# A log-sum-exp kernel: block-ordered rows and one closing store for the last batch, late sums in its last tiles, one common store for the other batches

## The chip, the cores and the metric

The kernel runs on one core of one Trainium2 chip. The metric is the device time of one execution in microseconds (us). Twelve executions of the kernel before gave a median of 335.04 us, from 333.62 to 335.29. The profiled execution took 334.2 us, of which the span from the first to the last profiled instruction is 332.4 us; the 1.8 us between the two lie outside the profile.

## What is computed

The input x has 8 batches of 2048 rows of 2048 floats, 134 MB in all. A row holds 8 heads of 256 values; a bias (8 x 256) is added; for each row and head the output is log(sum(exp(x + bias))), and each result is written twice in a row.

```python
x_heads = x.reshape(B, S, H, Dh).transpose(0, 2, 1, 3)
x_heads = x_heads + bias[None, :, None, :]
x_tiled = np.repeat(x_heads, 2, axis=2)
mx = x_tiled.max(axis=-1, keepdims=True)
lse = mx.squeeze(-1) + np.log(np.exp(x_tiled - mx).sum(axis=-1))
```

The output is 8 x 8 x 4096 floats, 1.05 MB. The kernel does not subtract the maximum; it sums exp(x + bias), or exp(x) * exp(bias), directly.

## The kernel before

**Tiles.** A tile is 256 rows of one batch as 128 partitions x K = 2 rows x 2048 columns, 2 MB. There are T = 64 tiles, eight per batch, and nine buffers `xt`. Tile t lives in buffer t mod 9. `rows_of` (L94) gives partition p the two neighbouring rows 2p and 2p + 1, one run of 16 KB in memory, except in the very last tile, where row k of partition p is row k * 128 + p. `load` (L102) issues the load from the SP queue. `next_waiting` (L340) calls it for tile t + 9 once tile t has been read.

**Stages.** `STAGES` (L27) sets how a tile's eight heads are split, and whether the load and the work go by whole tiles or by halves of 1 MB (one row k at a time):

- tiles 0 to 48, BULK: heads 0 and 1 by the TensorE path, heads 4 to 7 by the GpSimd path, heads 2 and 3 by a weight; whole tiles
- tiles 49 to 56, MIXED: head 0 by TensorE, heads 1 to 4 by weights, heads 5 to 7 by GpSimd; whole tiles
- tiles 57 to 60: MIXED in halves
- tiles 61 to 63, PROMPT: heads 0 and 1 by TensorE, heads 2 to 7 by weights, nothing on GpSimd; in halves

The last tile is cut further by `LAST_CUTS` (L29): its first half is one piece; its second half has pieces of columns 0 to 1024, 1024 to 1536 and 1536 to 2048.

**Paths.** On the TensorE path `add_bias` (L159) puts the bias into PSUM with one matmul of a row of ones (L166), adds the tile with a matmul against the identity (L171), and `sum_biased` (L174) lets ScalarE take exp and sum over each head (L177, an ACTIVATE and an ACTIVATION_READ_ACCUMULATOR per head). On the GpSimd path `g_add` (L195) adds the bias in place, ScalarE takes exp (L200), and VectorE sums (L216). On the weight path ScalarE takes exp of x alone (L200), and `weigh` (L228) multiplies by exp(bias) and sums, one instruction pair per head on VectorE; BULK does the same with one multiplication for two heads (L210) ahead of the reduction.

**Order of the work.** The order is written out by hand: the main loop (L302) issues, for each piece, the TensorE work and the GpSimd addition, then what `waiting` holds of the piece before (its exp and VectorE sums of the GpSimd heads, and the load of tile t + 9), then the exp of the weighted heads, the sums of its TensorE heads, and the weighing. Each engine runs its instructions in the order of issue. DMA issues from SP rotate over eight completion semaphores, and an issue waits until the DMA eight issues earlier has landed.

**Ends of batches.** The sums of a batch lie in `R[b]` (rows on partitions). `finish_batch` (L283) transposes them with TensorE (L244, two transposes into `tpair`), takes Ln into one of two buffers `res` (L257; the repetition comes from reading each value twice), and stores 64 partitions x 2 KB (128 KB) from the SP queue (L278). It runs two tiles after the batch's last tile, and stands in the same SP queue as the loads. The last batch is finished in four parts: tiles 56 to 61 (`R7`: 48 rows, eight stores of 12 KB from the GpSimd queue), tile 62 (`Ry`, 16 KB), and each half of tile 63 (`Rz`, 8 KB each), the last after everything else (L356).

Of the kernel before, what the change touches and what calls it, by code (L numbers as in the profile page):

```python
# [9 lines left out]
F32 = mybir.dt.float32  # L10
BF16 = mybir.dt.bfloat16
ACT = mybir.ActivationFunctionType
# [3 lines left out]
K = 2  # L16
# [9 lines left out]

STAGES = [(0, BULK, False), (49, MIXED, False), (57, MIXED, True), (61, PROMPT, True)]  # L27

LAST_CUTS = [[0, 2048], [0, 1024, 1536, 2048]]  # L29


@with_exitstack
def kernel(
# [6 lines left out]
    nc = tc.nc  # L40
    P = nc.NUM_PARTITIONS
    B, S, D = x.shape
    H, Dh = bias.shape
    assert D == H * Dh and S % (P * K) == 0
    NBLK = S // (P * K)
    T = B * NBLK
    CPE = 2 * Dh
    MM = 512
# [3 lines left out]
    sb = ctx.enter_context(tc.tile_pool(name="sb", bufs=1))  # L52
# [7 lines left out]
    ident = sb.tile([P, P], F32, name="ident")  # L60
    ones = sb.tile([1, P], F32, name="ones")
    ones3 = sb.tile([3, P], BF16, name="ones3")
    b3 = sb.tile([3, CPE], BF16, name="b3")
    bparts = sb.tile([1, 3, CPE], BF16, name="bparts")
    brest = sb.tile([1, 2, CPE], F32, name="brest")

    nblk = [NBLK] * (B - 1) + [NBLK - 2]
    R = [sb.tile([P, K, H, nblk[b]], F32, name=f"R{b}") for b in range(B)]
    Ry = sb.tile([P, K, H], F32, name="Ry")
    Rz = sb.tile([P, K, H], F32, name="Rz")  # L70
    junk = [sb.tile([P, Dh], F32, name=f"junk{i}") for i in range(2)]
    res = [sb.tile([H * NBLK, P, K, 2], F32, name=f"res{i}") for i in range(2)]
    xts = [sb.tile([P, K, D], F32, name=f"xt{i}") for i in range(NBUF)]
    w_ps = pp.tile([P, W1 - W0], F32, name="w_ps")
    ps = [pp.tile([P, MM], F32, name=f"ps{i}") for i in range(5)]
# [1 line left out]
    tps = [tpair[:, i] for i in range(2)]  # L77

    def mode_of(t):
        return [m for t0, m, _ in STAGES if t0 <= t][-1]  # L80
# [4 lines left out]
    def pieces(t):  # L85

        if not halves_of(t):
            return [(0, K, 0, D)]
        cuts = [[0, D]] * K if t < T - 1 else LAST_CUTS
        return [  # L90
            (k, k + 1, c0, c1) for k in range(K) for c0, c1 in zip(cuts[k], cuts[k][1:])
        ]

    def rows_of(t):  # L94

        b, blk = divmod(t, NBLK)
        v = x[b, blk * P * K : (blk + 1) * P * K, :]
        if t < T - 1:
            return v.rearrange("(p k) d -> p k d", k=K)
        return v.rearrange("(k p) d -> p k d", k=K)  # L100

# [10 lines left out]
    for set_idx, (_name, funcs) in enumerate(get_activation_tables(nc.m.arch).items()):  # L112
        if ACT.Exp in funcs and ACT.Ln in funcs:
            nc.scalar.add_instruction(
                mybir.InstLoadActFuncSet(
                    name=nc.get_next_instruction_name(),
# [27 lines left out]
    for i, c in enumerate(range(G0, D, MM)):  # L144
        spread(ps[i], c, c + MM)
        nc.scalar.activation(  # L146
            out=b_rep[:, c - G0 : c - G0 + MM], in_=ps[i], func=ACT.Copy
# [8 lines left out]
    n_ps = [0]  # L156
    n_junk = [0]

    def add_bias(m, views):  # L159

        n = m["pe"] * Dh
        got = []
        for v in views:
            p = ps[n_ps[0] % len(ps)]
            n_ps[0] += 1
            nc.tensor.matmul(  # L166
                p[:, 0:n], lhsT=ones3, rhs=b3[:, 0:n], start=True, stop=False
            )
            got.append(p)
        for p, v in zip(got, views):  # L170
            nc.tensor.matmul(p[:, 0:n], lhsT=ident, rhs=v, start=False, stop=True)  # L171
        return got

    def sum_biased(m, p, dst):  # L174
        for h in range(m["pe"]):
            c = h * Dh
            nc.scalar.activation(  # L177
                out=p[:, c : c + Dh],
                in_=p[:, c : c + Dh],
                func=ACT.Exp,  # L180
                accum_out=dst(h),
            )

    def each_row(src, c, n, k_rows):

        return bass.AP(
            tensor=src.tensor,
            offset=src.offset + c,
            ap=[src.ap[0], [0, k_rows], [1, n]],
        )  # L190

    def g_add(m, xt, k0, k1):
        c = m["g0"] * Dh
        v = xt[:, k0:k1, c:D]
        nc.gpsimd.tensor_tensor(  # L195
            out=v, in0=v, in1=each_row(b_rep, c - G0, D - c, k1 - k0), op=ALU.add
        )

    def exp_inplace(v):
        nc.scalar.activation(out=v, in_=v, func=ACT.Exp)  # L200
# [22 lines left out]
    def weigh(v, h, dst):  # L223
        c = h * Dh
        w = w_ps[:, c - W0 : c - W0 + Dh] if c < W1 else w_sb[:, c - W1 : c - W1 + Dh]
        j = junk[n_junk[0] % 2]
        n_junk[0] += 1
        nc.vector.tensor_tensor_reduce(  # L228
            out=j,
            in0=v,  # L230
            in1=w,
            scale=1.0,
            scalar=0.0,
            op0=ALU.mult,
            op1=ALU.add,
            accum_out=dst,
        )

    def finish(b, src, n_blk, k_rows, base, i, engine):

        nr = H * n_blk
        n = P * k_rows * 2
        for k in range(k_rows):
            nc.tensor.transpose(out=tps[i][0:nr, k], in_=src(k), identity=ident)  # L244
        tp = tps[i]
        rs = res[i]
        tv = bass.AP(
            tensor=tp.tensor,
            offset=tp.offset,
            ap=[[tp.ap[0][0], nr], [1, P], [P, k_rows], [0, 2]],  # L250
        )
        rv = bass.AP(
            tensor=rs.tensor,
            offset=rs.offset,
            ap=[[rs.ap[0][0], nr], [2 * k_rows, P], [2, k_rows], [1, 2]],
        )
        nc.scalar.activation(out=rv, in_=tv, func=ACT.Ln)  # L257

        if n_blk == 1:
            step, parts = 2 * S, [H]  # L260
        elif n_blk == NBLK:
            step, parts = n, [nr]
        else:
            step, parts = n, [n_blk] * H
        r0 = 0
        for rows in parts:
            h, m = divmod(r0, n_blk)
            ov = bass.AP(
                tensor=out.tensor,
                offset=out.offset + (b * H + h) * 2 * S + 2 * base + m * n,  # L270
                ap=[[step, rows], [1, n]],
            )
            iv = bass.AP(
                tensor=rs.tensor,
                offset=rs.offset + r0 * rs.ap[0][0],
                ap=[[rs.ap[0][0], rows], [1, n]],
            )
            engine.dma_start(out=ov, in_=iv)  # L278
            r0 += rows
        assert r0 == nr  # L280


    def finish_batch(b, engine):  # L283
        finish(
            b,
            lambda k: R[b][:, k].rearrange("p h n -> p (h n)"),
            nblk[b],
            K,
            0,
            b % 2,  # L290
            engine,
        )

    def sums_of(t):

        b, blk = divmod(t, NBLK)
        if t < T - 2:
            return R[b][:, :, :, blk]
        return Ry if t < T - 1 else Rz

    waiting = None
    for t in range(T):  # L302
        m = mode_of(t)
        xt = xts[t % NBUF]
        sums = sums_of(t)
        with_pool = m["g0"] < H
        for k0, k1, c0, c1 in pieces(t):
            if t == T - 1 and c1 == D and k0 > 0:

                finish(  # L310
                    B - 1,
                    lambda k: Rz[:, k0 - 1],
                    1,
                    1,
                    S - (K - k0 + 1) * P,
                    0,
                    nc.sync,
                )
            if c0 == 0:
                got = add_bias(m, [xt[:, k, 0 : m["pe"] * Dh] for k in range(k0, k1)])  # L320
                if with_pool:
                    g_add(m, xt, k0, k1)

            if waiting:
                waiting()
            h0 = max(c0 // Dh, m["pe"])
            h1 = min(c1 // Dh, m["g0"])
            if h0 < h1 and not m["late"]:
                exp_inplace(xt[:, k0:k1, h0 * Dh : h1 * Dh])
            if c0 == 0:  # L330
                for k in range(k0, k1):
                    sum_biased(m, got[k - k0], lambda h: sums[:, k, h : h + 1])
            if not m["late"]:
                for k in range(k0, k1):
                    for h in range(h0, h1):
                        weigh(
                            xt[:, k, h * Dh : (h + 1) * Dh], h, sums[:, k, h : h + 1]
                        )

            def next_waiting(t=t, m=m, xt=xt, k0=k0, k1=k1, sums=sums):  # L340
                if m["g0"] < H:
                    later(m, xt, k0, k1, sums)
                if k1 == K and t + NBUF < T:
                    load(t + NBUF)

            waiting = next_waiting
            if t == T - 1 and c0 == 0:
                if k0 == 0:
                    finish_batch(B - 1, nc.gpsimd)
                elif k0 == 1:  # L350
                    finish(B - 1, lambda k: Ry[:, k], 1, K, S - 2 * K * P, 0, nc.sync)

        fb, at = divmod(t - 2, NBLK)
        if fb >= 0 and at == NBLK - 1:
            finish_batch(fb, nc.sync)
    finish(B - 1, lambda _: Rz[:, K - 1], 1, 1, S - P, 1, nc.sync)  # L356

    order.__exit__(None, None, None)

# [29 lines left out]
```

## Time and profile before

| | |
|---|---|
| profiled execution | 334.2 us; span 332.4 us |
| median of 12 executions | 335.04 us (333.62 to 335.29) |
| VectorE busy | 288.6 us, 87% of the span |
| ScalarE busy | 291.7 us, 88% |
| GpSimd busy | 274.6 us, 83% |
| TensorE busy | 229.2 us, 69%, at a mean granted clock of 0.73 |
| DMA | 135.43 MB at a mean of 407 GB/s; HBM read 134.23 MB, written 1.05 MB |
| chain that ended last | DMA 65%, ScalarE 15%, TensorE 10%, GpSimd 4% of the span |

A busy share is an average over the whole span, so it says nothing of what limits a given stage. The chain that ended last is followed back from the last instruction, each time to what released the waiting instruction. Wherever it says "DMA xt<-in_x_dram", an engine had been waiting for a load; a long chain of engine lines means that the engines followed one another with no load to wait for. In timelines, the number in brackets is the idle time ahead of an instruction, and the arrow names what ended it. The profile's trace also keeps every DMA packet (its start, its duration and its size) and the time at which each of the 16 DMA engines reported its share of a transfer as landed.

### The profile page before, as it was taken

The numbers are of one execution on the slowest core, as the hardware profiler recorded it, in microseconds if no ns is written. First come the engines' busy times: TensorE is split into PE (matmuls) and PEld (weight loads), VectorE is DVE, ScalarE is ACT, GpSimd is POOL, SyncE is SP. The second block draws the span as 40 slices with busy tenths as digits, with TensorE's granted clock in tenths as the row PEclk, the third lists the DMA queues.
The fourth block names the chain that finished last, engine by engine and source line by source line (L and its number), as shares of the span: only waits on it lengthen the run. The fifth ranks groups of instructions, "written<-read, shape, count | busy, mean of one in ns | idle before, by whom it ended". The sixth has DMA issues, their size and how long they took to land.

```text
span 332.4 us, 2370 instructions
## 1 busy us (share of the span) xinstructions
PE 229.2 (69%) x412; PEld 71.8 (22%) x412; DVE 288.6 (87%) x380; ACT 291.7 (88%) x570; POOL 274.6 (83%) x87
## 2 busy tenths in 40 slices
PE   6496774796766766776968856778774554665981
PEld 2122221221221221221222221121122232222220
DVE  0029999999999999899989999999899999999992
ACT  2279999899999999989899999998999987899893
POOL 7999989998989999999898999988997766876204
PEclk9999777559798769877595789865876555555576
DMA  7999999999999999999999999999999999999940
GB/s 293 436 436 420 433 424 432 432 422 432 425 429 425 430 426 425 436 425 428 429 428 424 434 426 430 428 426 433 428 424 431 428 428 428 413 422 420 421 175 17
DMA packets 11489, 135.43 MB, mean 407 GB/s; under 512 B 1609, under 2 KB 1625, under 8 KB 2513
## 3 DMA queue, kind: packets, MB, share of 16 engines
q1 hardware_dynamic: 11120, 135.17, 96.1%
q0 software_dynamic: 352, 0.10, 0.2%
q14 instruction: 12, 0.10, 0.1%
q8 instruction: 3, 0.05, 0.1%
q10 hardware_dynamic: 2, 0.01, 0.0%
HBM read 134.23 MB, written 1.05 MB: 407 GB/s over the span
## 4 chain that ended last, share of the span: by engine, by line
DMA 65%; ACT 15%; PE 10%; POOL 4%; issue 2%; DVE 2%; POOLq 0%; DVEq 0%; SPq 0%; ACTq 0%
DMA xt<-in_x_dram 63%; ACT xt L200 10%; PE ps L171 8%; ACT ps L177 5%; POOL xt L195 3%; DMA b<-bparts 2%; PE ps L166 1%; DVE R L216 1%; DVE xt L210 1%; DMA brow<-in_bias_dram 1%; DMA out_dram<-res 0%; PE tpair L244 0%; DVE junk L228 0%; POOL brest L131 0%; POOL brest L133 0%
## 5 line engine op out<-in xcount | busy, mean ns | idle before, releaser
L195 POOL TENSOR_TENSOR xt<-xt,b_rep 128x2048 f32<-128x2048 f32 (+2 forms) x65 | 264.2, 4066 | 36.3 <-DMA xt<-in_x_dram 30.1
L171 PE MATMUL ps<-xt,ident 128*128 128x512 f32 (+1 forms) x256 | 174.7, 819 | 76.9 <-DMA xt<-in_x_dram 75.5
L200 ACT ACTIVATE xt<-xt 128x3072 f32<-128x3072 f32 (+3 forms) x89 | 184.8, 2095 | 11.4 <-POOL xt L195 11.1
L216 DVE TENSOR_REDUCE R<-xt 128x12 f32<-128x3072 f32 (+2 forms) x65 | 186.0, 2861 | 5.8 <-DVE xt L210 1.0
L177 ACT ACTIVATE ps<-ps 128x256 f32<-128x256 f32 x232 | 85.6, 369 | 16.1 <-PE ps L171 11.7
L171 PEld LDWEIGHTS ps<-xt,ident 128*128 128x128 f32 x256 | 59.2, 259 | 157.4 <-DMA xt<-in_x_dram 115.5
L210 DVE TENSOR_TENSOR xt<-xt,w_ps 128x1024 f32<-128x1024 f32 x49 | 59.6, 1217 | 30.0 <-ACT xt L200 29.8
L166 PE MATMUL ps<-b,ones 3*128 3x512 bf16 (+1 forms) x128 | 48.2, 449 | 8.3 <-ACT ps L177 4.8
L177 ACT ACTIVATION_READ_ACCUMULATOR ps<-ps 128x1 f32 x232 | 44.1, 190 | 0.0
L228 DVE CUSTOM_DVE_ANT_0 junk<-xt,w_ps 128x256 f32<-128x256 f32 x114 | 40.6, 415 | 2.6 <-ACT xt L200 2.5
L166 PEld LDWEIGHTS <-ones 3*128 3x128 bf16 x128 | 8.0, 98 | 72.2 <-issue 72.2
L278 POOL DMA_DIRECT2D out_dram<-res x8 | 4.0, 505 | 14.2 <-ACT res L257 14.2
L244 PE MATMUL tpair<-ident,R 128*64 128x128 f32 (+1 forms) x16 | 4.4, 369 | 7.0 <-DVE R L216 7.0
L228 DVE DVE_READ_ACCUMULATOR2_ANT R<- 128x1 f32 x108 | 8.9, 82 | 0.0
L257 ACT ACTIVATE res<-tpair 64x512 f32<-64x512 f32 (+3 forms) x11 | 5.9, 540 | 2.7 <-PE tpair L244 1.6
L228 DVE CUSTOM_DVE_ANT_0 junk<-xt,w_sb 128x256 f32<-128x256 f32 x18 | 6.8, 421 | 1.2 <-ACT xt L200 1.2
L140 PE MATMUL ps<-brow,ones 1*128 1x512 f32 x4 | 3.7, 1089 | 2.9 <-DMA brow<-in_bias_dram 2.9
L244 PEld LDWEIGHTS tpair<-ident,R 128*64 128x64 f32 (+1 forms) x16 | 1.9, 143 | 14.9 <-DVE R L216 12.7
L146 ACT ACTIVATE b_rep<-ps 128x512 f32<-128x512 f32 x2 | 1.2, 597 | 4.1 <-PE ps L140 4.1
L140 PE MATMUL w_ps<-brow,ones 1*128 1x512 f32 x4 | 4.0, 1096 | 0.7 <-ACT w_ps L152 0.7
L152 ACT ACTIVATE w_ps<-w_ps 128x512 f32<-128x512 f32 x2 | 1.2, 582 | 3.3 <-PE w_ps L140 3.3
L244 PE MATMUL tpair<-ident,Rz 128*8 128x128 f32 x2 | 0.6, 323 | 4.5 <-DVE Rz L228 3.1
(23 smaller groups left out, 14.1 us busy)
## 6 DMA issues: line engine op xcount, KB each, us to landing
xt<-in_x_dram SPq DMA_DIRECT2D x57, 2048.0 KB, 31.8
xt<-in_x_dram SPq DMA_DIRECT2D x13, 1024.0 KB, 20.3
out_dram<-res SPq DMA_DIRECT2D x7, 128.0 KB, 31.9
xt<-in_x_dram SPq DMA_DIRECT2D x1, 512.0 KB, 18.6
xt<-in_x_dram SPq DMA_DIRECT2D x2, 256.0 KB, 15.9
out_dram<-res POOLq DMA_DIRECT2D x8, 12.0 KB, 1.7
b<-bparts POOLq DMA_DIRECT2D x3, 1.0 KB, 5.6
out_dram<-res SPq DMA_DIRECT2D x2, 8.0 KB
```

The lines of the kernel that those rows point to most:

```text
L140: nc.tensor.matmul(dst, lhsT=ones, rhs=brow[:, c0:c1], start=True, stop=True)
L166: nc.tensor.matmul(p[:, 0:n], lhsT=ones3, rhs=b3[:, 0:n], start=True, stop=False)
L171: nc.tensor.matmul(p[:, 0:n], lhsT=ident, rhs=v, start=False, stop=True)
L177: nc.scalar.activation(out=p[:, c : c + Dh], in_=p[:, c : c + Dh], func=ACT.Exp, accum_out=dst(h),)
L195: nc.gpsimd.tensor_tensor(out=v, in0=v, in1=each_row(b_rep, c - G0, D - c, k1 - k0), op=ALU.add)
L200: nc.scalar.activation(out=v, in_=v, func=ACT.Exp)
L210: nc.vector.tensor_tensor(out=f, in0=f, in1=each_row(w_ps, h0 * Dh - W0, n, k1 - k0), op=ALU.mult,)
L216: nc.vector.tensor_reduce(out=sums[:, k0:k1, h0:H], in_=v.rearrange("p k (h j) -> p k h j", j=Dh), op=ALU.add, axis=mybir.AxisListType.X,)
L228: nc.vector.tensor_tensor_reduce(out=j, in0=v, in1=w, scale=1.0, scalar=0.0, op0=ALU.mult, op1=ALU.add, accum_out=dst,)
L244: nc.tensor.transpose(out=tps[i][0:nr, k], in_=src(k), identity=ident)
L257: nc.scalar.activation(out=rv, in_=tv, func=ACT.Ln)
L278: engine.dma_start(out=ov, in_=iv)
```

## The change

Four edits come together.

1. The results of batches 0 to 6 stay in one buffer `res` (64 partitions x 7 x 2 KB). Their transposes and Ln remain where they were. One store of 896 KB from the SP queue, issued after the Ln of batch 6 (in the loop's pass for tile 57), takes the place of seven stores of 128 KB.
2. The last batch loads all its tiles with row k * 128 + p on partition p, and its sums go to one tile `R_last` (head, block, k). `finish_last` ends it after everything else with one transpose of 128 x 128, one Ln of 128 x 256 and one SP store of 128 partitions x 1 KB (128 KB). The four separate ends of the last batch are gone, with their six transposes, four Lns and eleven stores.
3. In tiles 61 to 63 the exp-and-sum of the TensorE heads (`pe_part`) is put off: it stands behind the exp of the next piece that begins or ends a row instead of ahead of the weighing of its own. The cuts of the last tile become 0, 512, 1280, 2048 and 0, 512, 1536, 2048, so that each half begins with a piece of just the two TensorE heads.
4. In tiles 49 to 56, where the TensorE path has one head, the two rows of a tile share one PSUM buffer and one pair of matmuls of 512 columns in the place of two pairs of 256.

The order of instructions on each engine otherwise stays; VectorE has the same instructions in the same order.

```diff
-LAST_CUTS = [[0, 2048], [0, 1024, 1536, 2048]]
+LAST_CUTS = [[0, 512, 1280, 2048], [0, 512, 1536, 2048]]
...
+    R = [sb.tile([P, K, H, NBLK], F32, name=f"R{b}") for b in range(B - 1)]
+    R_last = sb.tile([P, H, NBLK, K], F32, name="R_last")
...
+    res = sb.tile([H * NBLK, B - 1, P, K, 2], F32, name="res")
+    res_last = sb.tile([P, P, 2], F32, name="res_last")
...
-        if t < T - 1:
+        if b < B - 1:
             return v.rearrange("(p k) d -> p k d", k=K)
         return v.rearrange("(k p) d -> p k d", k=K)
...
+        nc.scalar.activation(out=res[:, b], in_=tv, func=ACT.Ln)
+
+    def store():
+
+        nc.sync.dma_start(
+            out=out[0 : B - 1].rearrange("b h (n r) -> (h n) b r", n=NBLK),
+            in_=res.rearrange("q b p k r -> q b (p k r)"),
+        )
+
+    def finish_last():
+        tp = tps[(B - 1) % 2][:, 0]
+        nc.tensor.transpose(
+            out=tp, in_=R_last.rearrange("p h n k -> p (h n k)"), identity=ident
+        )
...
+        nc.scalar.activation(out=res_last, in_=tv, func=ACT.Ln)
+        nc.sync.dma_start(
+            out=out[B - 1].rearrange("h (n r) -> (h n) r", r=2 * P),
+            in_=res_last.rearrange("q p r -> q (p r)"),
+        )
...
+            if for_pool:
+                for_pool()
+                for_pool = None
             h0 = max(c0 // Dh, m["pe"])
             h1 = min(c1 // Dh, m["g0"])
             if h0 < h1 and not m["late"]:
                 exp_inplace(xt[:, k0:k1, h0 * Dh : h1 * Dh])
-            if c0 == 0:
-                for k in range(k0, k1):
-                    sum_biased(m, got[k - k0], lambda h: sums[:, k, h : h + 1])
+            if for_pe and (c0 == 0 or c1 == D):
+                for_pe()
+                for_pe = None
...
+            for_pool = pool_part
+            if c0 == 0:
+                if m["g0"] < H:
+                    pe_part()
+                else:
+                    for_pe = pe_part
...
         if fb >= 0 and at == NBLK - 1:
-            finish_batch(fb, nc.sync)
-    finish(B - 1, lambda _: Rz[:, K - 1], 1, 1, S - P, 1, nc.sync)
+            finish(fb)
+            if fb == B - 2:
+                store()
+    for_pe and for_pe()
+    finish_last()
```

More of the change, by code (lines that the diff above doesn't have):

```diff
@@ L65 @@
     brest = sb.tile([1, 2, CPE], F32, name="brest")
[L67 to L70, printed above, removed]
+    R = [sb.tile([P, K, H, NBLK], F32, name=f"R{b}") for b in range(B - 1)]
+    R_last = sb.tile([P, H, NBLK, K], F32, name="R_last")
     junk = [sb.tile([P, Dh], F32, name=f"junk{i}") for i in range(2)]
-    res = [sb.tile([H * NBLK, P, K, 2], F32, name=f"res{i}") for i in range(2)]
+    res = sb.tile([H * NBLK, B - 1, P, K, 2], F32, name="res")
+    res_last = sb.tile([P, P, 2], F32, name="res_last")
     xts = [sb.tile([P, K, D], F32, name=f"xt{i}") for i in range(NBUF)]
@@ L157, with add_bias @@
     n_junk = [0]
-    def add_bias(m, views):
+    def add_bias(m, xt, k0, k1):
         n = m["pe"] * Dh
+        step = MM // n
+        groups = [(k, min(k + step, k1)) for k in range(k0, k1, step)]
         got = []
-        for v in views:
+        for ka, kb in groups:
             p = ps[n_ps[0] % len(ps)]
@@ L166, in add_bias @@
             nc.tensor.matmul(
-                p[:, 0:n], lhsT=ones3, rhs=b3[:, 0:n], start=True, stop=False
-            )
-            got.append(p)
-        for p, v in zip(got, views):
-            nc.tensor.matmul(p[:, 0:n], lhsT=ident, rhs=v, start=False, stop=True)
+                p[:, 0 : (kb - ka) * n],
+                lhsT=ones3,
+                rhs=each_row(b3, 0, n, kb - ka),
+                start=True,
+                stop=False,
+            )
+            got += [p[:, k * n : (k + 1) * n] for k in range(kb - ka)]
+        for ka, kb in groups:
+            p = got[ka - k0]
+            nc.tensor.matmul(
+                bass.AP(tensor=p.tensor, offset=p.offset, ap=[p.ap[0], [1, (kb - ka) * n]]),
+                lhsT=ident,
+                rhs=xt[:, ka:kb, 0:n],
+                start=False,
+                stop=True,
+            )
         return got
@@ L237, in weigh, with finish @@
         )
[L239 to L246, printed above, removed]
+    def finish(b):
+        nr = H * NBLK
+        tp = tps[b % 2]
+        for k in range(K):
+            nc.tensor.transpose(
+                out=tp[0:nr, k],
+                in_=R[b][:, k].rearrange("p h n -> p (h n)"),
+                identity=ident,
+            )
         tv = bass.AP(
@@ L249, in finish @@
             offset=tp.offset,
-            ap=[[tp.ap[0][0], nr], [1, P], [P, k_rows], [0, 2]],
+            ap=[[tp.ap[0][0], nr], [1, P], [P, K], [0, 2]],
         )
[L252 to L255, printed above, removed]
-        )
[L257 to L291, printed above, removed]
+        nc.scalar.activation(out=res[:, b], in_=tv, func=ACT.Ln)
[3 more added lines that the diff above has]
+            in_=res.rearrange("q b p k r -> q b (p k r)"),
+        )
+    def finish_last():
+        tp = tps[(B - 1) % 2][:, 0]
+        nc.tensor.transpose(
+            out=tp, in_=R_last.rearrange("p h n k -> p (h n k)"), identity=ident
+        )
+        tv = bass.AP(
+            tensor=tp.tensor, offset=tp.offset, ap=[tp.ap[0], [1, P], [0, 2]]
+        )
+        nc.scalar.activation(out=res_last, in_=tv, func=ACT.Ln)
+        nc.sync.dma_start(
+            out=out[B - 1].rearrange("h (n r) -> (h n) r", r=2 * P),
+            in_=res_last.rearrange("q p r -> q (p r)"),
         )
@@ L296, in sums_of @@
         b, blk = divmod(t, NBLK)
-        if t < T - 2:
+        if b < B - 1:
             return R[b][:, :, :, blk]
-        return Ry if t < T - 1 else Rz
-    waiting = None
+        return R_last[:, :, blk, :].rearrange("p h k -> p k h")
+    for_pool = for_pe = None
     for t in range(T):
@@ L305 @@
         sums = sums_of(t)
-        with_pool = m["g0"] < H
         for k0, k1, c0, c1 in pieces(t):
[L308 to L318, printed above, removed]
             if c0 == 0:
-                got = add_bias(m, [xt[:, k, 0 : m["pe"] * Dh] for k in range(k0, k1)])
-                if with_pool:
+                got = add_bias(m, xt, k0, k1)
+                if m["g0"] < H:
                     g_add(m, xt, k0, k1)
-            if waiting:
-                waiting()
+            if for_pool:
+                for_pool()
+                for_pool = None
             h0 = max(c0 // Dh, m["pe"])
@@ L338, with pool_part @@
                         )
-            def next_waiting(t=t, m=m, xt=xt, k0=k0, k1=k1, sums=sums):
+            def pool_part(t=t, m=m, xt=xt, k0=k0, k1=k1, sums=sums):
                 if m["g0"] < H:
@@ L344, in next_waiting, with pe_part @@
                     load(t + NBUF)
[L346 to L351, printed above, removed]
+            def pe_part(m=m, got=got, k0=k0, k1=k1, sums=sums):
+                for k in range(k0, k1):
+                    sum_biased(m, got[k - k0], lambda h: sums[:, k, h : h + 1])
+            for_pool = pool_part
+            if c0 == 0:
+                if m["g0"] < H:
+                    pe_part()
+                else:
+                    for_pe = pe_part
         fb, at = divmod(t - 2, NBLK)
         if fb >= 0 and at == NBLK - 1:
-            finish_batch(fb, nc.sync)
-    finish(B - 1, lambda _: Rz[:, K - 1], 1, 1, S - P, 1, nc.sync)
+            finish(fb)
[3 more added lines that the diff above has]
+    finish_last()
     order.__exit__(None, None, None)
```

## The prediction

> **What bounds the kernel now.** I read the page's slices first, then its DMA issues. In the slices each digit is a fortieth of the span (8.3 us) in tenths; below it are GB/s.
>
> ```profile
> DMA  7999999999999999999999999999999999999940
> GB/s 293 436 436 420 433 424 432 432 422 432 425 429 425 430 426 425 436 425 428 429 428 424 434 426 430 428 426 433 428 424 431 428 428 428 413 422 420 421 175 17
> ...
> xt<-in_x_dram SPq DMA_DIRECT2D x57, 2048.0 KB, 31.8
> ...
> out_dram<-res SPq DMA_DIRECT2D x7, 128.0 KB, 31.9
> out_dram<-res POOLq DMA_DIRECT2D x8, 12.0 KB, 1.7
> ```
>
> The DMA engines are full from the second slice to the 38th, at about 427 GB/s. A load lands 31.8 us after its issue although 2 MB take 4.9 us: six tiles are queued ahead of it. So the stream of loads, not its issue, sets the pace, and whatever else is in its queue delays it. The seven stores of 128 KB are in it: 31.9 us to land, like a load. The GpSimd queue's small stores run when the loads are over: 1.7 us.
>
> The second thing is the end. Loads land, by the trace's landing records, until 322.40 us; the span ends at 332.43. The windows view gives the engines around it (length, busy us with instruction counts on PE, PEld, DVE, ACT, POOL, then granted TensorE clock, DMA share, GB/s):
>
> ```profile
> 262.00:287.00 25.00, 13.42 (x31) 6.88 (x32) 25.00 (x97) 21.54 (x32) 17.50 (x6) 0.50 1.00 424
> 287.00:310.00 23.00, 15.04 (x32) 6.08 (x31) 23.00 (x92) 21.37 (x39) 17.63 (x9) 0.50 1.01 421
> 310.00:322.00 12.00, 10.86 (x16) 2.76 (x16) 11.06 (x59) 10.99 (x23) 0.00 (x0) 0.64 0.80 323
> 322.00:333.00 11.00, 3.09 (x8) 0.94 (x7) 4.12 (x24) 4.94 (x15) 3.98 (x8) 0.66 0.06 14
> ```
>
> After 322 no engine is half busy: the end is a chain of waits. VectorE is full from 262 to 310, which a rival below takes up. The last links, from the chain of waits in order of time (start, us, what):
>
> ```profile
> 325.24 0.48 ACT res L257
> 325.72 0.02 issue
> 325.74 1.50 DMA out_dram<-res
> 327.24 0.02 issue
> 327.26 0.02 ACTq L257
> 327.27 0.04 issue
> 327.32 0.09 ACT res L257
> 327.41 0.19 issue
> 327.60 0.62 ACT xt L200
> 328.22 0.02 issue
> 328.24 0.42 DVE junk L228
> ```
>
> ScalarE's Ln at 327.32 waits for a store to leave the buffer `res` that it reuses (1.50 us), and the exp of the last piece, whose data were there at 322.40, stands behind it until 327.60.
>
> **Edit 1, the seven stores become one.** From the packet records: a store's 2 KB packet takes 84 ns (median), a load's 16 KB packet 613. A store of 64 rows reports 16 landings, so each DMA engine does 4 packets: 4 x 84 = 0.34 us; the first landing of a store is 0.29 to 0.31 us behind the load before it, and the next load follows at the normal step. I take 0.30 us. Six of the seven stores are ahead of the last load (issued at 65 to 262 us), the seventh (309.99) behind: 6 x 0.30 = 1.80 us sooner. The one store has 448 packets, 28 per engine: 28 x 84 = 2.35 us behind the last load of each engine. It waits for the Ln of batch 6 and for the landing of tile 62's first half, so it is issued near 313, when every load is already issued; only the final store is queued behind it on SP. Issuing it costs SP between 0.5 us (a store now) and seven times that, with nothing due on SP until 325.
>
> Two rules of the Trainium skill bear on this. "DMA: Bandwidth & Descriptors", section "Rules for kernel authors", says to issue a DMA early and wait for it late, so that its fixed cost is hidden. By it, early stores are free, moving them gains nothing, and the end could only get later. The row speaks otherwise: with the queue full, a store's packets take the loads' places. By the rule the move is worth 0, by the row 1.80 us; I take the row. The same page's section "Anatomy of one DMA — SWDGE (gpsimd) path" fits 2.0 us + bytes / 436 GB/s; that would be an estimate of 4.1 us for 917,504 bytes, from another queue kind, against 2.35 us by the row. Even 4.1 us from the slowest engine's last load (320.8, below) ends at 324.9, ahead of the final store.
>
> **Edit 2, the last batch's rows and its end.** Tile 56 comes in 8 KB packets, not 16 KB: 8 x (2 x 312 - 613) = +0.09 us per engine; the halves have 8 KB packets already. The last tile's new pieces: before, 8 packets per engine of 8, 4, 2 and 2 KB, i.e. 8 x (312 + 159 + 84 + 84) = 5.11 us; after, 2, 3, 3, 2, 4, 2 KB. The trace has no 3 KB packet; it lies between 84 and 159 ns, I take the middle, 122: 8 x (3 x 84 + 2 x 122 + 159) = 5.24, +0.13 (between -0.5 and +0.7). So the last load lands at 322.40 - 1.80 + 0.09 + 0.13 = 320.82, and tile 62's second half at 317.39 - 1.71 = 315.7. Gone are the Lns of 0.48 us between the last pieces, the wait for `res`, and eleven stores; the eight of GpSimd end at 328.75 and held nobody up.
>
> **Edit 3, the sums put off.** Nothing is added; ScalarE no longer waits for TensorE within a unit. Now tile 61's first sums wait 0.55 us for the matmuls (L171, two of 1.04 us at the granted clock 0.5 to 0.64); put off, they find it done. PSUM has five buffers and two are in use, so no matmul waits for the later reading. The exp of the next piece is queued ahead of the sums, the weighing follows that exp at once.
>
> ScalarE's steps from start to start in the timeline of 310 to 330: exp of 1536 columns 1.37 us, two sums 0.89, exp of 512 0.48; in between by length, 768: 0.70, 1024: 0.92. In the order after, with tile 62's second half landed at 315.7:
>
> - exp 1536: 315.75 to 317.1; sums of tile 62's halves: 318.0, 318.9
> - last tile, first half (landed by 318.3): two exps of 768 to 320.3, sums to 321.2
> - second half: exp 1024 (landed 320.2) to 322.1, exp 512 (landed 320.8) to 322.6, sums to 323.5
>
> VectorE weighs a head in 0.343 us: from 322.15 six heads are 2.06, plus 0.08 for the last accumulator read: 324.3. It is the later one. TensorE at the old pace of 2.54 us per half ends by 323.0.
>
> What follows the last weighing is taken from before: VectorE ends at 329.02, transpose 329.17, Ln 329.58, store 329.98, landing 331.28, end 332.43: 3.41 us. The transpose is 128 x 128 as before; Ln of 256 columns is 0.37 us whether for 8 rows or, I assume, 128 (64x512 takes 578 ns and 8x512 569). The store is 128 KB where it was 8: 8 packets of 1 KB per engine at 62 ns, +0.5 us (between 0 and 1.0; a 12 KB store takes 1.7). End: 324.3 + 3.41 + 0.5 = 328.2.
>
> **Edit 4, two rows in one matmul.** In tiles 49 to 56 the first sum waits for the matmuls of both rows. At 271.93 these start and end at 274.0; ScalarE comes to the first sum at 273.82, so it waits 0.2 us per tile. I take 0, since ScalarE then idles 0.8 us for GpSimd in every such tile (3.5 us in 25); without that cover it would be 8 x 0.2 = 1.6 us. A saving on TensorE is worth 0 there too (13.42 busy of 25).
>
> **Sum.** Span 332.43 to 328.2: -4.2 us, of which 1.6 from loads landing sooner (1.80 - 0.22) and 2.6 from the shorter end. The profiled execution goes from 334.2 to 330.0. It lies 0.84 under the median of the runs, so against 335.04 the changed kernel's median is 335.04 - 4.2 = 330.84, say 330.8.
>
> **Rivals.**
>
> *VectorE holds the landing gain back.* It is full from 254.6 to 314 us, so loads that land sooner in that stretch find it busy. Against: the stretch opens with an idle 0.17 us behind a load of tile 48 that moves by 1.2 us (four stores), and it works a tile off in 4.44 us against 4.95 of landing; started 1.2 sooner, it is level at tile 62's second half, by 317.15. If the gain were lost whole, -2.6: 332.4. Chance 0.11.
>
> *Store packets are dear when they are many.* Eight 2 KB packets of a late store took up to 252 ns. At 250 ns, 28 take 7.0 us: 320.8 to 327.8; the final store queues behind, lands near 328.6, span 329.8, -2.6: 332.4. Against: 712 packets in the full queue had a median of 84. Chance 0.08.
>
> *Slower: the common store is spread over few engines.* 448 packets on k engines take 448 x 84 / k ns from about 320.8: k = 16: 2.35 us, k = 4: 9.4, which ends the span near 332.3, as now; from k = 3 down it is slower, and at k = 2 (18.8 us) the median is about 344. For it: the change makes a shape of 64 x 7 x 512 that no row shows. Against: the 64-row stores report on 16 engines, and the same page, section "Why a DMA increments its semaphore by 16 and not by 1", sets the number by the slowest dimension of both sides, here still 64. The same end would follow from packets of over 360 ns. Chance 0.03.
>
> *The change does not do what it says*: the new end gives back what it saves, because landings spread (the last DMA engine is 4.0 us behind the first at the end, in steps of 0.7 to 1 us where an instruction fetch of 8 KB runs on that engine) and four such steps fall badly. About 335. Chance 0.03.
>
> **How the numbers follow.** The forecast has 0.75. Its own bounds: the closing store -0.5 to +0.5, piece sizes -0.6 to +0.6, one fetch step on the slowest engine either way 0.9, sums waiting for TensorE 0 to +0.9. Together 329.6 to 332.0. The first two rivals widen it to 332.7. A measurement tells about 0.2% (0.7 us) from no change: faster 0.94, within 0.03, slower 0.03.
>
> **What would show it.** Landing of the last load near 320.8 and DMA slices without stores; one store of 896 KB landing by 323.5 on 16 engines; ScalarE unbroken from about 315.7 to 323.5; a tail of about 4 us from the last weighing to the end. Wrong if the last load lands as late as 322, if VectorE is still behind when tile 63 lands, or if the final store waits for the common one.

## The result, and the profile after

The changed kernel takes 329.83 us (median of 8 executions, 329.65 to 330.01) where the kernel before, over all the executions timed by then, takes 334.96 (333.62 to 335.31). The ratio is 0.9849, with a 95% interval of 0.984 to 0.9857: 5.1 us faster. The forecast was 330.8 us, in a range of 329.6 to 332.7. The profiled execution took 329.83 us with a span of 328.1 (forecast: 330.0 and 328.2).

Two rows and two DMA issues from the page after:

```profile
DMA  7999999999999999999999999999999999999991
GB/s 301 424 434 428 428 431 426 436 424 424 432 425 433 426 428 428 425 433 428 429 426 426 432 428 428 428 428 431 428 430 427 426 432 422 416 423 419 420 375 41
...
out_dram<-res SPq DMA_DIRECT2D x1, 896.0 KB, 10.7
...
out_dram<-res_last SPq DMA_DIRECT2D x1, 128.0 KB, 1.7
```

The DMA engines are full as before. The 39th slice (311.7 to 319.9 us) now holds the last loads and, behind them, most of the common store of 896 KB (375 GB/s). This store landed 10.7 us after its issue, at 323.76; the closing store took 1.7 us.

The last link of the chain of waits, in order of time (start, us, what):

```profile
322.11 0.42 DVE junk L240
...
324.25 0.02 DVE R_last L240
324.27 0.14 issue
324.41 0.46 PE tpair L277
324.87 0.02 issue
324.89 0.38 ACT res_last L283
```

The Lns and the wait for a result buffer between the last pieces are gone. VectorE's six heads, one transpose and one Ln follow one another. ScalarE's timeline of the same stretch (start, us; the bracket is the idle time ahead):

```profile
320.14 0.37 ACT L189 ACTIVATE ps<-ps 128x256 f32<-128x256 f32 x1
...
320.66 0.37 ACT L189 ACTIVATE ps<-ps 128x256 f32<-128x256 f32 x1
...
321.03 1.56 ACT L212 ACTIVATE xt<-xt 128x1024 f32<-128x1024 f32 x2
322.50 0.37 ACT L189 ACTIVATE ps<-ps 128x256 f32<-128x256 f32 x1
...
324.89 0.38 ACT L283 ACTIVATE res_last<-tpair 128x256 f32<-128x256 f32 x1 [1.40 <-PE tpair L277]
```

Up to the last Ln no instruction has a bracket: from 315.51, when it takes up tile 62's second half (landed at 315.48), ScalarE waits for nothing until its sums are done at 323.49. The two instructions at 321.03 are the exps of 1024 and of 512 columns.

### The profile page after: what moved, and what is told of

It reads as the page before. It is cut to its first block, busy times and chain, and to the rows that moved or that the text cites. A ratio compares the mean times of both kernels' runs of the same rounds, so it can differ in the third digit from the quotient of the medians.

```text
span 328.1 us, 2272 instructions
## 1 busy us (share of the span) xinstructions
PE 231.6 (71%) x383; PEld 66.6 (20%) x383; DVE 288.1 (88%) x380; ACT 291.2 (89%) x567; POOL 270.6 (82%) x79
## 4 chain that ended last, share of the span: by engine, by line
DMA 65%; ACT 15%; PE 7%; POOL 6%; DVE 5%; issue 2%; POOLq 0%; SPq 0%; DVEq 0%
DMA xt<-in_x_dram 63%; ACT xt L212 10%; PE ps L177 5%; ACT ps L189 4%; POOL xt L207 4%; DVE R L228 3%; DMA b<-bparts 2%; PE ps L167 1%; DVE xt L222 1%; DVE junk L240 1%; DMA brow<-in_bias_dram 0%; POOL brest L132 0%; POOL brest L130 0%; POOL b L135 0%; PE tpair L256 0%
## 5 line engine op out<-in xcount | busy, mean ns | idle before, releaser
L177 PE MATMUL ps<-xt,ident 128*128 128x512 f32 (+1 forms) x240 | 177.3, 871 | 72.1 <-DMA xt<-in_x_dram 71.4
L228 DVE TENSOR_REDUCE R<-xt 128x12 f32<-128x3072 f32 (+1 forms) x56 | 176.6, 3154 | 5.8 <-DVE xt L222 1.0
L189 ACT ACTIVATE ps<-ps 128x256 f32<-128x256 f32 x232 | 85.7, 369 | 15.1 <-PE ps L177 10.7
L177 PEld LDWEIGHTS ps<-xt,ident 128*128 128x128 f32 x240 | 54.6, 257 | 150.8 <-DMA xt<-in_x_dram 110.0
L256 PE MATMUL tpair<-ident,R 128*64 128x128 f32 x14 | 4.0, 380 | 8.5 <-DVE R L228 7.1
L228 DVE TENSOR_REDUCE R_last<-xt 128x3 f32<-128x768 f32 (+1 forms) x9 | 9.3, 1031 | 0.0
L240 DVE DVE_READ_ACCUMULATOR2_ANT R_last<- 128x1 f32 x76 | 5.8, 76 | 0.0
L256 PEld LDWEIGHTS tpair<-ident,R 128*64 128x64 f32 x14 | 1.6, 141 | 14.6 <-DVE R L228 11.1
L240 DVE DVE_READ_ACCUMULATOR2_ANT R<- 128x1 f32 x56 | 4.3, 77 | 0.0
L266 ACT ACTIVATE res<-tpair 64x512 f32<-64x512 f32 x7 | 4.0, 578 | 0.1
## 6 DMA issues: line engine op xcount, KB each, us to landing
out_dram<-res SPq DMA_DIRECT2D x1, 896.0 KB, 10.7
```

Source lines behind the costliest of these rows:

```text
L177: nc.tensor.matmul(bass.AP(tensor=p.tensor, offset=p.offset, ap=[p.ap[0], [1, (kb - ka) * n]]), lhsT=ident, rhs=xt[:, ka:kb, 0:n], start=F ...
L189: nc.scalar.activation(out=p[:, c : c + Dh], in_=p[:, c : c + Dh], func=ACT.Exp, accum_out=dst(h),)
L228: nc.vector.tensor_reduce(out=sums[:, k0:k1, h0:H], in_=v.rearrange("p k (h j) -> p k h j", j=Dh), op=ALU.add, axis=mybir.AxisListType.X,)
L240: nc.vector.tensor_tensor_reduce(out=j, in0=v, in1=w, scale=1.0, scalar=0.0, op0=ALU.mult, op1=ALU.add, accum_out=dst,)
L256: nc.tensor.transpose(out=tp[0:nr, k], in_=R[b][:, k].rearrange("p h n -> p (h n)"), identity=ident,)
L266: nc.scalar.activation(out=res[:, b], in_=tv, func=ACT.Ln)
```

## The experiments

Times are medians. The last column compares all executions with those of the kernel before in the same set (what was timed together), whose median was 334.96 us for the changed kernel, 334.62 from before_again to end_only, 335.09 from after_again to finer_cuts, and 334.62 for the last two. It is not the quotient of the two medians; where the kernel before spreads widely, the two can differ (end_only: 0.9956 by the medians).

| run | us (from, to) | ratio to before (95%) |
|---|---|---|
| changed kernel | 329.83 (329.65, 330.01) | 0.9849 (0.984, 0.9857) |
| before_again | 334.76 (333.37, 335.28) | 1.0004 (0.9985, 1.0024) |
| stores_early | 332.35 (332.01, 332.62) | 0.9936 (0.992, 0.9951) |
| store_only | 333.38 (331.87, 333.64) | 0.9954 (0.9936, 0.9973) |
| end_only | 333.15 (332.0, 334.1) | 0.9968 (0.995, 0.9985) |
| after_again | 329.9 (329.79, 329.93) | 0.9849 (0.9832, 0.9866) |
| no_defer | 331.58 (330.46, 332.54) | 0.99 (0.9879, 0.9921) |
| pairs | 329.9 (329.64, 329.94) | 0.9848 (0.9831, 0.9865) |
| finer_cuts | 329.41 (329.28, 329.51) | 0.9835 (0.9818, 0.9853) |
| dummy_loads | 339.37 (339.0, 340.01) | 1.0153 (1.0124, 1.0181) |
| stores_late7 | 329.94 (329.92, 330.32) | 0.9871 (0.9849, 0.9894) |

**The kernel before, again (before_again, before_third, before_fourth).** No edit; more traces, to find what the forecast's 0.84 us between the profiled execution and the median stood for.

> The kernel before once more, to have a second trace of it. The forecast's sum was right for the profiled execution (span 332.4 to 328.2 forecast, 328.1 measured), but the median fell by 5.1 us, not 4.2, since the profiled execution before lay 0.8 us under its own median. Theory A: the usual execution before has its last load land later on the slowest DMA engine, by about 0.8 us (near 323.2 against 322.4), and the same 10.0 us from there to the end. Theory B: the last load lands near 322.4 as well, and the chain behind it is longer, about 10.8 us.

The second trace was of an even shorter execution, 333.4 us (span 331.6). Its last load landed at 322.61, 0.2 us later than in the first trace, while the end came 0.8 us sooner. So landing does not set the difference between executions. The two later traces:

> The kernel before, one more trace, in the hope of one of its usual executions of about 335. Theory: then the granted clock is 0.5 from 316 to 324, the matmul pairs of the last tile take 2.0 us each and ScalarE's sums wait for both, 1 to 1.5 us in all, where the traces of 334.2 and 333.4 show waits of 0.50 and 0; the last load lands where it did, near 322.5. Rival: the last load lands later.

> As before_third: a fourth trace of the kernel before, with the same two readings.

before_third was short again: 333.26 us, last load at 322.49. before_fourth caught a usual execution: 334.96 us (span 333.2), last load at 322.46, and 10.7 us from there to the end. ScalarE's waits for TensorE in the last tile, and then TensorE's matmul pairs, in before_fourth:

```profile
322.07 0.37 ACT L177 ACTIVATE ps<-ps 128x256 f32<-128x256 f32 x1 [0.28 <-PE ps L171]
...
325.04 0.37 ACT L177 ACTIVATE ps<-ps 128x256 f32<-128x256 f32 x1 [0.99 <-PE ps L171]
```

```profile
319.96 2.07 PE L171 MATMUL ps<-xt,ident 128*128 128x512 f32 x2
...
322.92 2.08 PE L171 MATMUL ps<-xt,ident 128*128 128x512 f32 x2
```

The same pairs in before_again, then ScalarE's one wait for them in the first trace:

```profile
320.11 1.13 PE L171 MATMUL ps<-xt,ident 128*128 128x512 f32 x2 [0.59 <-DMA xt<-in_x_dram]
...
321.70 1.13 PE L171 MATMUL ps<-xt,ident 128*128 128x512 f32 x2
```

```profile
324.26 0.37 ACT L177 ACTIVATE ps<-ps 128x256 f32<-128x256 f32 x1 [0.50 <-PE ps L171]
```

A pair takes 2.07 us at a granted clock of 0.5 and 1.13 at full clock. The clock came back at 316.8 (for 3.4 us), 319.0, 318.6 and 325.0 us in the four traces (before, before_again, before_third, before_fourth); the last of these is too late for the last tile, and ScalarE's sums waited 0.28 and 0.99 us there, against none and 0.50 in the first trace, and none in before_again and before_third. With the last load within 0.2 us in all four traces, theory B of the expectation holds: the usual execution has the longer chain. Only one of the four traces is of a usual execution; no_defer below tests the same wait by an edit.

**Stores early (stores_early).** The changed kernel with edit 1 undone.

```diff
             finish(fb)
-            if fb == B - 2:
-                store()
+            nc.sync.dma_start(
+                out=out[fb].rearrange("h (n r) -> (h n) r", n=NBLK),
+                in_=res[:, fb].rearrange("q p k r -> q (p k r)"),
+            )
```

> The changed kernel with the seven stores back in their old places, 128 KB each after each batch's Ln. Theory (a store in the full queue takes the loads' places, 0.30 us each, six of them ahead of the last load): 1.8 us slower than the changed kernel, about 331.6. Rival (VectorE, full from 255 to 314, holds the gain of earlier landings back, or the queue hides stores): as the changed kernel, 329.8.

332.35 us: 2.5 us slower than the changed kernel, more than the 1.8 expected, and far from the rival. In the traces, tile 62's second half landed 1.77 us later on the DMA engine that was first (313.61 against 311.84), 1.88 on the eighth of the sixteen, 1.59 on the last; the last weighing ended 1.6 us later. That is the forecast's price of six stores. The span is 2.2 us longer, since between the last landing and the end there are 1.6 us in place of 1.0: SP's closing sequence has two more semaphore waits behind the last landing (0.06 to 0.1 us each) and a pause of 0.34 us. The remaining 0.3 to 0.4 us between trace and median is not explained.

**The common store alone (store_only).** The kernel before with edit 1:

```diff
-            finish_batch(fb, nc.sync)
+            finish_kept(fb)
+            if fb == B - 2:
+                store()
```

Here `finish_kept` does what `finish(b)` does in the changed kernel: transposes, and the Ln into a buffer for all seven batches.

> The kernel before with edit 1 alone: one store of 896 KB for batches 0 to 6 after the Ln of batch 6; everything else as before. Theory: 1.8 us faster than before, about 333.2. Rival (the landing gain is held back by VectorE or by the end's own chain): 335.0. Should the common store delay the small stores of the last batch's end that stand behind it in the queue, the gain shrinks: the first of them is issued near 324, the common store ends near 323.

333.38 us, 1.2 us by the medians (334.62 in its set). Its executions form two groups, 331.87 to 332.5 and 333.25 to 333.64; those of the kernel before in this set lie all along from 333.38 to 335.31. The shortest fell by 1.5 us (333.38 to 331.87) and the longest by 1.7 (335.31 to 333.64), near the theory's 1.8. VectorE did not hold the landing gain back.

**The new end alone (end_only).** The kernel before with edit 2:

```diff
-        if t < T - 1:
+        if b < B - 1:
             return v.rearrange("(p k) d -> p k d", k=K)
...
-    finish(B - 1, lambda _: Rz[:, K - 1], 1, 1, S - P, 1, nc.sync)
+    finish_last()
```

The other three ends of the last batch are taken out as well, in lines not shown.

> The kernel before with edit 2 alone: rows of the last batch in blocks of 128, one transpose, one Ln and one store at its end; seven early stores, sums not put off, old cuts of the last tile. Theory: the two Lns between the last pieces, the wait for the result buffer and the transposes go; last weighing near 326.5 instead of 329.0, closing store 0.5 us dearer: about 2.0 us faster than before, 333.0. Rival (the gain of the end comes from the put-off sums and the new cuts, edit 3): within 0.5 us of before, 334.5 to 335.

333.15 us, 1.5 us faster than before (334.62) by the medians, 1.1 by the ratio (0.5 to 1.7): between the theory's 2.0 and the rival's 0.5 at most. So the new end is worth something alone, but not all of what was forecast for it. The executions still spread over 2.1 us. In its trace (333.45 us) ScalarE waits 0.36 and 0.64 us for TensorE at the last tile's two sums: with the Lns gone, the sums still stand behind the matmuls.

**The sums in their old place (no_defer).** The changed kernel, and beside it the changed kernel once more:

```diff
             if c0 == 0:
-                if m["g0"] < H:
-                    pe_part()
-                else:
-                    for_pe = pe_part
+                pe_part()
```

> The changed kernel once more, beside the others of this set on one chip. Same median as before, 329.8, and, by the theory of the next run (its end no longer waits for TensorE), a spread of its executions of under 0.6 us where the kernel before spreads over 1.9.

> The changed kernel with the sums of tiles 61 to 63 ahead of the next exp again (edit 3 without its postponement, with its new cuts). Theory: the median of the kernel before lies above its two profiled executions (334.2, 333.4) because the end waits for TensorE, and the two traces differ in when the granted clock came back from one half: pairs of matmuls of 1.1 or of 2.0 us while the last tile was worked. Sums that wait for TensorE bring that back: 0.4 to 1.3 us slower than the changed kernel (330.2 to 331.1) and a wider spread, over 0.8 us. Rival (the spread comes from where instruction fetches delay the slowest DMA engine): time within 0.2 us and the narrow spread of the changed kernel.

after_again spread over 0.14 us; no_defer over 2.1, with a median 1.7 us higher: the theory's sign, at more than its size. ScalarE in no_defer's trace:

```profile
317.87 0.37 ACT L189 ACTIVATE ps<-ps 128x256 f32<-128x256 f32 x1 [0.56 <-PE ps L177]
...
320.41 0.37 ACT L189 ACTIVATE ps<-ps 128x256 f32<-128x256 f32 x1 [1.56 <-PE ps L177]
```

The first piece of the last tile now holds only TensorE's heads, so sums in their old place have nothing in front of them: they wait 1.56 us for a pair at half clock. This trace is of the slowest of the six executions (332.54); at the fastest, the sums' place costs 0.7 us (330.46 against 329.79). In after_again's trace the clock was as bad, and nothing waited for it. The windows view of after_again (length; busy us and counts of PE, PEld, DVE, ACT, POOL; granted clock; DMA share; GB/s):

```profile
316.00:320.00 4.00, 4.00 (x5) 0.75 (x4) 3.43 (x21) 3.94 (x11) 0.00 (x0) 0.50 0.91 344
320.00:324.00 4.00, 1.56 (x4) 0.39 (x3) 3.51 (x21) 3.50 (x11) 0.00 (x0) 0.92 0.12 45
```

The clock is 0.50 until 320, TensorE is full, and ScalarE is busy 3.94 of 4 us. The execution took 329.88 us.

**Two pairs of matmuls (pairs).** The changed kernel with edit 4 undone:

```diff
-        step = MM // n
+        step = 1
```

> The changed kernel with two pairs of matmuls of 256 columns per tile in tiles 49 to 56 (edit 4 undone). Forecast's step: worth 0, so 329.8. Rival: the 0.2 us of waiting per tile that the joint matmul costs is not covered, 8 x 0.2, so 1.6 us faster than the changed kernel at most, 328.2; or TensorE's saving counts, then slower.

329.9 us, as after_again in the same set. The edit is worth nothing, as forecast.

**Finer cuts (finer_cuts).**

```diff
-LAST_CUTS = [[0, 512, 1280, 2048], [0, 512, 1536, 2048]]
+LAST_CUTS = [[0, 512, 1280, 2048], [0, 512, 1024, 1536, 2048]]
```

> The changed kernel with the last half cut at 512, 1024, 1536 columns, so that VectorE can start its last six heads after an exp of 512 columns, not of 1024. Theory (after the last load's landing the six heads of 2.06 us on VectorE end the work, and they start when the first exp of the half is through): that exp starts at 321.03 and takes 0.48 instead of 0.95, so VectorE ends 0.5 us sooner: 329.3. Rival (the landing of the last pieces sets the start, and one more piece costs 0.1 us): 329.8 to 329.9.

329.41 us, 0.5 us faster than after_again (329.9), with no overlap between the executions of the two. The last accumulator read starts at 323.66 instead of 324.18. It is the fastest kernel here.

**Extra loads in the stores' places (dummy_loads).**

```diff
             finish(fb)
+            if fb < B - 2:
+                nc.sync.dma_start(
+                    out=spare, in_=x[fb, 0 : H * NBLK, 0 : 2 * K * P]
+                )
```

> The changed kernel with six extra loads of 128 KB (64 partitions x 2 KB of x, into a tile that nobody reads) in the SP queue at the places where the first six stores were; 0.79 MB more are read, nothing else differs. Theory (the price of an early store is the DMA engines' time for its packets, 0.30 us each, and every end moves with the loads): 1.8 us slower than the changed kernel, 331.7. Rival (part of the 2.5 us that the early stores cost belongs to writing to memory or to the chain at the end): 1.0 us or less, 330.9.

A miss on both sides: 339.37 us, 9.5 slower than the changed kernel. The page's GB/s row has dips that no other trace has:

```profile
GB/s 304 431 429 425 430 429 427 431 421 433 392 423 427 433 417 383 433 426 431 424 379 429 425 431 427 365 433 426 423 412 391 425 425 423 381 410 419 416 318 29
```

Tile 62's second half landed 9.4 us later than in the changed kernel (324.88 against 315.48), so the whole cost is in the stream of loads, 1.6 us for each extra load. Their own packets are the smaller part: 384 of them at 108 ns on average, against a store's 85, are 2.6 us on each of 16 engines. The larger part is in their neighbours: while an extra load is in flight the tiles' 16 KB packets take up to 1.33 us instead of 0.61 (from 130 to 133 us the mean of each microsecond is 0.70 to 1.08 us), and over the whole run the tiles' 16 KB and 8 KB packets took 5.4 us more per engine than in the changed kernel. The remaining 1.4 us of the 9.4 are not accounted for. Why a load of 64 partitions x 2 KB slows its neighbours, when a store of the same shape does not, is open: the runs don't separate the reading (2 KB of each of 64 neighbouring rows) from the writing to 64 partitions. The run says nothing on the price of a store.

**Seven late stores (stores_late7).** The changed kernel's `store()` as a loop of seven:

```diff
-        nc.sync.dma_start(
-            out=out[0 : B - 1].rearrange("b h (n r) -> (h n) b r", n=NBLK),
-            in_=res.rearrange("q b p k r -> q b (p k r)"),
-        )
+        for i in range(B - 1):
+            nc.sync.dma_start(
+                out=out[i].rearrange("h (n r) -> (h n) r", n=NBLK),
+                in_=res[:, i].rearrange("q p k r -> q (p k r)"),
+            )
```

> The changed kernel with seven stores of 128 KB issued one after the other where it issues the one of 896 KB. Theory (what pays is that they are late, not that they are one): the same packets behind the loads, the last store lands by 324, before the closing store is issued at 325.3: 329.8 to 330.0. Rival (many stores are dear: each waits for one of the eight completion semaphores): the closing store waits, over 330.5.

329.94 us. In the trace the last of the seven landed at 323.32; the closing store is issued at 325.59, when the data are ready, and waits for no other. So what pays is that the stores are late, not that they are one.

## Why the prediction was right, point by point

**The loads' gain: right, but for the last load.** Forecast: tile 62's second half lands at 315.7, measured 315.48. Over the DMA engines the last load came 1.3 (first), 1.6 (eighth) and 0.8 us (last) sooner; the forecast was 1.58. On the slowest engine two of the last pieces, 1.0 us apart on the first engine, land at 317.33 and 319.02; an instruction fetch of 8 KB at 316.74 falls together with this slip. So the last load landed at 321.57, not at 320.8; the forecast had allowed for such a step, with 0.9 us. It cost nothing, and that was luck: the piece of 1024 columns landed at 320.94 and ScalarE came to it at 321.03. The undoing in stores_early shows the 1.6 to 1.9 us at the load's landing; the gain is of lateness (stores_late7).

**The common store: right.** Issued at 313.02 (forecast "near 313"), spread over 16 engines, first share landed 2.39 us behind its engine's last load (forecast 2.35), last at 323.76 (forecast 323.2), before the closing store's issue at 325.30. The rule of the Trainium skill, "DMA: Bandwidth & Descriptors", section "Rules for kernel authors", to issue a DMA early, was rightly set aside: by it the early stores would have cost nothing, and in stores_early they cost 2.5 us. With a full queue and an end that leaves the DMA engines idle, late is the cheap place.

**The end: right in its order and its times.** Sums done at 323.49 (forecast 323.5), last weighing at 324.26 (324.3), from there to the end 3.80 us (3.91): span 328.06, forecast 328.2. In particular VectorE was level at tile 62's second half, though barely: it was done with the half before at 316.93, the exp that it needed next ended at 316.99, and its first weighing there began at 317.02. Had this half alone landed sooner, it would have had to wait for VectorE.

**The step that was mis-sized: from the profiled execution to the median.** The forecast took 4.2 us off the profiled execution and off the median alike ("It lies 0.84 under the median of the runs, so against 335.04 the changed kernel's median is 335.04 - 4.2"). That treated 0.84 us as a constant. By the four traces it is a property of the kernel before: how late TensorE's clock comes back. Edit 3 was priced by the waits of a trace in which the clock was back at 316.8, and removes them also where it comes back too late: from the usual execution of before_fourth the span fell by 333.2 - 328.1 = 5.1 us, the measured gain. The forecast listed "sums waiting for TensorE 0 to +0.9" as a risk of the kernel after; it was a cost of the kernel before. The mechanism of edit 3 was right and its size 0.8 us short. The range had no term for this; that the median still fell inside it, 0.2 us above its lower end, was luck. The rows of granted clock, of the first trace and of before_fourth, differ in the last two slices, where the last tile is worked:

```profile
PEclk9999777559798769877595789865876555555576
...
PEclk9999798585977858789576577785857555555557
```

A digit between 5 and 9 says that the clock changes within the slice; the question is then whether it does so at the same time in every execution.

**The rivals.** VectorE holding the gain back would have shown in store_only and stores_early; neither does. Dear store packets and few engines are refuted by the landings above, and an end that gives back what it saves by the time itself. What the parts are worth by the medians: store alone 1.2, end alone 1.5, sums undone 1.7. These need not add up to 5.1, since the first two are tried on the kernel before and the third on the changed one. In the set of no_defer everything but the postponement takes 335.09 to 331.58, and the postponement takes that to 329.9. The new cuts were not tried alone.

## What to carry to other kernels

When a queue is full until the last load, anything in it that need not be early is paid in full; put it behind the last load, if what follows leaves the DMA engines idle long enough to hide it. Before a median is forecast from one trace, ask what differs between executions of the kernel before: an edit that takes a fluctuating engine off the path is worth its usual cost, not its cost in that trace. A narrow spread (0.14 to 0.6 us in the kernels whose sums are put off, 1.0 in dummy_loads with its slowed loads, against 1.7 to 2.1 in the others) is itself a sign that such a wait is gone.

## What the runs showed of the hardware that was not expected

The granted clock changes in steps of 3.4 us: its stretches near the end of the four traces of the kernel before last 3.4, 6.8, 10.2, 64.9 and 71.7 us, which are 1, 2, 3, 19 and 21 such steps. The Trainium skill, "TensorE: Matmul & The Clock Gate", Part 1, says that the gate decides by a free-running window of 3.4 us, so that the same program meets it in a different phase each time; the spread of the kernel before agrees. But that page grants the full clock after about one busy window, and here it took longer. In the four traces TensorE is busy, as the profile counts it, with no gap over 0.03 us from a start between 309.6 and 310.0 until the clock is back, and that takes 6.8, 9.4, 8.9 and, in before_fourth, 15.3 us. By the page's figure the clock would have been back after two windows at most, 6.8 us (an estimate from its 3.4), near 316.5 in before_fourth, in time for the last tile; it was back at 325.0, and the execution took 334.96 us. The measurement decides; what the gate counts as busy was not tried.

A load of 128 KB to 64 partitions in a full queue cost 1.6 us, a store of the same shape 0.3. And SP's closing sequence behind the last landing took 1.0 us in the changed kernel and 1.6 in stores_early, whose closing store is the same: it had two more semaphores to test there, and one short pause.
